# Per-head RMS norm in the attention fronts: epsilon added by VectorE, rotation and learned factors on raw rows, the rms factor last, D's five heads rotated together

## The chip, the cores and the metric

One core of one Trainium2 chip. The metric is device time in microseconds (us) for one execution, median of three runs; times inside an execution come from one profiled execution of the hardware profiler. Engines: TensorE (PE, its weight loads PEld), VectorE (DVE), ScalarE (ACT), GpSimd (POOL), and the DMA queue that SyncE (SP) issues.

## The reference

Two layers of a hybrid encoder, sequence 512, width 1024, all float32. Each layer's mixer has four attention branches, each on its own projection of the normed input. All of them norm queries and keys per head before the scores:

```python
def rms(x, g):
    y = x * lax.rsqrt(jnp.mean(x * x, axis=-1, keepdims=True) + EPS)
    return y * g

# A, differential: 4 heads x 2 maps x 64     C, windowed, 8 query / 2 key heads of 64
q = rms(q, g_qk[0]); k = rms(k, g_qk[1])
# B, latent: rotated part of 32, plain part of 64, 8 heads
q_nope = rms(q[..., :64], g_qk[0, :64]); q_rope = rope(rms(q[..., 64:], g_qk[0, 64:]), pos)
k_nope = rms(kv[..., :64], g_qk[1, :64])
# D, two-axis rotation, 8 query / 2 key heads of 64
q = axial_rope(rms(q, g_qk[0]), row, col); k = axial_rope(rms(k, g_qk[1]), row, col)

def rope(x, pos):           # x1, x2: halves of the head
    return x * cos + concatenate([-x2, x1]) * sin
...
o = stack([o_a, o_b, o_c, o_d]); br = einsum('bsmc,mcd->bsmd', o, w_branch)
x = x + (sigmoid(gate) * br).sum(2) @ w_out
x = x + memory_xattn(...)                   # 4 heads, 256 memory tokens
x = x + square(relu(rms(x, g_mlp) @ w_up)) @ w_down
```

The factor 1/rms is one number per token and head. The rotation is linear within one head of one token, and the learned factors go by channel.

## The kernel before

Every large product is made of three matmuls (L177, L178, L179) on a rounded part and a rest of each operand. So each weight tile `wst` that arrives by DMA is split: ScalarE casts it to `whi` (L299), GpSimd subtracts to get `wlo` (L167, four instructions a tile). Activations are split the same way into `spl` tiles: a copy on ScalarE, a subtraction on VectorE (L167 too).

The mixer of a layer runs through twelve units in the order B 0 to 3, A 0 to 3, C 0 and 1, D 0 and 1. Each unit has a front and an attention; the front of the next unit is emitted behind the attention of the one before, with pieces of other work (gates and branch projections, tile `df`) between them as a string in the file deals them out. A front projects four blocks of 128 tokens (tile `dn`, 24 matmuls of 384 columns a block in A, C and D; 9 of 192 and 256 in B). ScalarE copies the block to a raw tile `tok` and squares it, VectorE sums the squares per head into `sf` (L415). Then come two halves of two blocks each: add epsilon (L311, in B L716 and L717) and raise to the power -0.5 (L312, in B L718) on GpSimd; on VectorE multiply by that factor (A L452, C and D L552, B L722 and L723), by the learned factors (A L454 with `ga`, D L557 with `gd`, B L725 and L727), rotate in B and D (the function `rope`: four products into tile `zr` at L584 or two in B, then L586 and L587); split into `spl` (copies on ScalarE, subtractions L167); TensorE transposes (L403, into `dn`), and the result is copied to `T` tiles (L172 on ScalarE, L174 on VectorE) as the scores need it. D rotates its four query heads and its key head in two calls.

The order of instructions on each engine is not that of the file: the framework's scheduler sets it when the program is built, from a simulated timeline, so that a shorter path at one place moves the rows of all engines around it. Each engine then runs its own rows in order and waits where an operand is missing.

## Time and profile before

| | before |
|---|---|
| runs, us | 2363.37, 2363.65, 2367.36; median 2363.65 |
| profiled execution, us | 2361.96 (span 2360.0 of it) |
| mean granted TensorE clock | 0.992 |
| TensorE busy | 2281.5 us, 97% |
| VectorE, ScalarE, GpSimd busy | 59%, 49%, 55% |
| data moved | 258.25 MB, mean 109 GB/s |

The span runs from the first to the last instruction of the profiled execution; 2 us lie outside it. Busy time counts an engine's instructions alone. A wait is given with what released it, as the semaphores show.

### The profile page before, as it was taken

The page shows a single profiled execution, that of the slowest core. Times are in us where ns is not written, and L with a number is a line of the kernel's source. Part 1 is how long each engine was busy: PE and PEld are TensorE (multiplying, and loading weights), DVE is VectorE, ACT ScalarE, POOL GpSimd, SP SyncE. Part 2 cuts the span into 40 slices and gives each one's busy share as a digit, 9 for nine tenths or more (in the row PEclk, how much of TensorE's full clock was granted, in tenths as well). Part 3 has the DMA queues.
Part 4 walks back from the last instruction along what each step waited for, and adds up shares of the span by engine and source line. Part 5 has one row for each costly group of instructions (what it writes and reads, how often), then busy time and mean ns, then how long its engine had stood idle before and what let it go on. Part 6 is the DMA issues. An engine that isn't in the chain of part 4 may idle for free.

```text
span 2360.0 us, 33643 instructions
## 1 busy us (share of the span) xinstructions
PE 2281.5 (97%) x12032; PEld 1966.0 (83%) x12032; DVE 1384.1 (59%) x2980; ACT 1151.8 (49%) x2253; POOL 1299.0 (55%) x1657
## 2 busy tenths in 40 slices
PE   8999999998999899999999998999989999999999
PEld 7888889887888888888888887898878878888887
DVE  7778666888975642222457786568879648222222
ACT  4556556655653543223345565566556546322321
POOL 7553544625465376666665435355353754766663
PEclk9999999999999999999999999999999999999999
DMA  5321342442454133333343214324425531323332
GB/s 185 108 94 57 102 138 66 127 154 84 147 179 155 54 99 98 98 92 96 111 134 101 83 46 127 113 79 134 136 92 168 171 131 56 106 91 97 98 93 77
DMA packets 88775, 258.25 MB, mean 109 GB/s; under 512 B 9704, under 2 KB 12392, under 8 KB 88608
## 3 DMA queue, kind: packets, MB, share of 16 engines
q1 hardware_dynamic: 88608, 256.10, 34.4%
q8 instruction: 95, 1.56, 0.3%
q14 instruction: 72, 0.59, 0.1%
HBM read 222.46 MB, written 33.60 MB: 109 GB/s over the span
## 4 chain that ended last, share of the span: by engine, by line
PE 83%; DVE 11%; POOL 2%; issue 1%; ACT 1%; DMA 1%; SPq 0%; POOLq 0%; ACTq 0%; DVEq 0%
PE dn L177 13%; PE dn L178 13%; PE dn L179 13%; PE df L177 10%; PE df L179 9%; PE df L178 9%; PE tr L476 3%; PE sc L177 1%; PE sc L179 1%; PE sc L178 1%; PE dn L403 1%; POOL wlo L167 1%; DVE pt L480 1%; DVE zr L584 1%; PE sc L624 1%
## 5 line engine op out<-in xcount | busy, mean ns | idle before, releaser
L167 POOL TENSOR_TENSOR wlo<-wst,whi 128x256 fp32r<-128x256 f32 (+3 forms) x1400 | 1071.0, 797 | 745.4 <-ACT whi L299 671.3
L299 ACT CAST whi<-wst 128x1024 fp32r<-128x1024 f32 (+3 forms) x350 | 348.8, 1003 | 640.8 <-PE dn L178 293.7
L177 PE MATMUL df<-s,whi 128*128 128x512 f32 (+1 forms) x967 | 381.0, 394 | 8.1 <-DVE zg L785 3.2
L179 PE MATMUL df<-s,wlo 128*128 128x512 f32 (+1 forms) x967 | 376.1, 389 | 1.3 <-POOL wlo L167 1.3
L178 PE MATMUL df<-s,whi 128*128 128x512 f32 (+1 forms) x967 | 374.3, 387 | 1.6 <-DVE s L167 1.6
L177 PE MATMUL dn<-whi,s 128*128 128x384 f32 (+4 forms) x768 | 264.8, 348 | 13.6 <-ACT s L348 7.7
L179 PE MATMUL dn<-whi,s 128*128 128x384 f32 (+4 forms) x768 | 263.3, 343 | 0.0
L178 PE MATMUL dn<-wlo,s 128*128 128x384 f32 (+4 forms) x768 | 263.1, 344 | 0.0
L177 PEld LDWEIGHTS df<-s,whi 128*128 128x128 f32 x967 | 181.7, 188 | 46.6 <-DVE yl L808 6.1
L179 PEld LDWEIGHTS df<-s,wlo 128*128 128x128 f32 x967 | 181.8, 188 | 38.4 <-POOL wlo L167 2.9
L178 PEld LDWEIGHTS df<-s,whi 128*128 128x128 f32 x967 | 181.9, 188 | 34.3 <-DVE s L167 2.2
L178 PE MATMUL dn<-s,whi 128*128 128x512 f32 (+1 forms) x529 | 197.1, 373 | 0.0
L179 PE MATMUL dn<-s,wlo 128*128 128x512 f32 (+1 forms) x529 | 196.9, 373 | 0.0
L177 PE MATMUL dn<-s,whi 128*128 128x512 f32 (+1 forms) x529 | 196.5, 374 | 0.0
L177 PEld LDWEIGHTS dn<-whi,s 128*128 128x128 f32 x768 | 146.8, 192 | 24.5 <-ACT s L348 7.7
L480 DVE TENSOR_TENSOR pt<-tr,pt 128x512 fp32r<-128x512 f32 (+1 forms) x224 | 142.7, 644 | 26.0 <-ACT pt L479 17.3
L178 PEld LDWEIGHTS dn<-wlo,s 128*128 128x128 f32 x768 | 147.2, 192 | 8.9 <-POOL wlo L167 0.2
L179 PEld LDWEIGHTS dn<-whi,s 128*128 128x128 f32 x768 | 146.8, 191 | 6.9
L479 ACT CAST pt<-tr 128x512 fp32r<-128x512 f32 (+1 forms) x224 | 121.8, 556 | 55.9 <-PE tr L476 54.3
L311 POOL TENSOR_SCALAR sf<-sf 128x8 f32<-128x8 f32 (+2 forms) x44 | 13.9, 316 | 241.3 <-DVE sf L415 239.5
L179 PEld LDWEIGHTS dn<-s,wlo 128*128 128x128 f32 x529 | 99.6, 188 | 17.9 <-POOL wlo L167 0.2
L178 PEld LDWEIGHTS dn<-s,whi 128*128 128x128 f32 x529 | 99.6, 188 | 17.8
(376 smaller groups left out, 4827.3 us busy)
## 6 DMA issues: line engine op xcount, KB each, us to landing
wst<-in_wts_dram SPq DMA_DIRECT2D x272, 512.0 KB, 3.5
wst<-in_wts_dram SPq DMA_DIRECT2D x64, 384.0 KB, 3.1
yl<-yz SPq DMA_DIRECT2D x48, 512.0 KB, 4.0
yz<-zg SPq DMA_DIRECT2D x64, 256.0 KB, 2.2
yz<-yl SPq DMA_DIRECT2D x48, 256.0 KB, 3.0
bias<-tscr SPq DMA_DIRECT2D x16, 320.0 KB, 3.3
yl<-yz SPq DMA_DIRECT2D x16, 256.0 KB, 3.1
bias<-tscr SPq DMA_DIRECT2D x8, 448.0 KB, 3.5
```

Source lines behind the costliest of these rows:

```text
L167: (eng or V).tensor_tensor(out=dst, in0=src, in1=f(hi), op=ALU.subtract)
L177: a = T.matmul(ps, lhsT=lh, rhs=rh, start=first, stop=False)
L178: T.matmul(ps, lhsT=lh, rhs=rl, start=False, stop=False)
L179: b = T.matmul(ps, lhsT=ll, rhs=rh, start=False, stop=last)
L299: chain("wh", A.copy(hi[:, :n], st[:, :n]))
L311: G.tensor_scalar(dst, src, add, None, op0=ALU.add)
L403: T.transpose(ps[:rows_, i * P:(i + 1) * P], s, idn)
L476: T.transpose(ps[:, kb * P:(kb + 1) * P], src[:, kb * P:(kb + 1) * P], idn)
L479: A.copy(hi, pv)
L480: V.tensor_tensor(out=lo, in0=pv, in1=f(hi), op=ALU.subtract)
L584: V.tensor_tensor(out=tmp[:, :, :, o:o + 16], in0=x[:, :, :, oo:oo + 16], in1=bc(tab[:, 1, b2, o:o + 16], 2, nh), op=ALU.mult)
L624: T.matmul(ps[:, :nk], lhsT=q, rhs=Tk[:, 0, kb0 * P:kb0 * P + nk], start=True, stop=False)
```

## The change

The epsilon adds of all fronts move from GpSimd to VectorE, and the power on GpSimd is emitted with a higher priority for the scheduler. In A, B and D the learned factors, and in B and D the rotation too, work on the raw rows; the multiplication by the per-head factor comes last, in C after the key's factor. D's five heads (four of queries, one of keys) are rotated in one call, for which tile `zr` grows from 512 to 640 columns.

```diff
     def rpow(dst, src, add, n):
-        G.tensor_scalar(dst, src, add, None, op0=ALU.add)
-        G.tensor_tensor(out=dst, in0=dst, in1=mhalf[:, :n], op=ALU.pow)
+        V.tensor_scalar(dst, src, add, None, op0=ALU.add)
+        with tc.high_priority():
+            G.tensor_tensor(out=dst, in0=dst, in1=mhalf[:, :n], op=ALU.pow)
...
     # front_A, half
-            V.tensor_tensor(out=qk, in0=qk, in1=bc(s.rearrange("p (t h) -> p t h", t=2), 3, 64), op=ALU.mult)
             for m in range(2):
                 V.tensor_tensor(out=kk[:, :, m], in0=kk[:, :, m], in1=bc(ga, 1, 2), op=ALU.mult)
+            V.tensor_tensor(out=qk, in0=qk, in1=bc(s.rearrange("p (t h) -> p t h", t=2), 3, 64), op=ALU.mult)
...
     # front_G (C and D), half
-            rpow(s, s, 64 * EPS, 10)
             qk = tk[:, :, :320].rearrange("p t (h d) -> p t h d", h=5)
-            V.tensor_tensor(out=qk, in0=qk, in1=bc(s.rearrange("p (t h) -> p t h", t=2), 3, 64), op=ALU.mult)
...
                 V.tensor_tensor(out=qk, in0=qk, in1=bc(gd, 1, 2), op=ALU.mult)
-                rope(qk[:, :, 0:4], dt_, j, 4, 2)
-                rope(qk[:, :, 4:5], dt_, j, 1, 2)
+                rope(qk, dt_, j, 5, 2)
+            rpow(s, s, 64 * EPS, 10)
+            V.tensor_tensor(out=qk, in0=qk, in1=bc(s.rearrange("p (t h) -> p t h", t=2), 3, 64), op=ALU.mult)
...
     # front_B
-            G.tensor_scalar(s3[:, :, 0:4], s3[:, :, 0:4], 64 * EPS, None, op0=ALU.add)
-            G.tensor_scalar(s3[:, :, 4:6], s3[:, :, 4:6], 32 * EPS, None, op0=ALU.add)
-            G.tensor_tensor(out=s, in0=s, in1=mhalf[:, :12], op=ALU.pow)
+            V.tensor_scalar(s3[:, :, 0:4], s3[:, :, 0:4], 64 * EPS, None, op0=ALU.add)
+            V.tensor_scalar(s3[:, :, 4:6], s3[:, :, 4:6], 32 * EPS, None, op0=ALU.add)
+            with tc.high_priority():
+                G.tensor_tensor(out=s, in0=s, in1=mhalf[:, :12], op=ALU.pow)
...
-            V.tensor_tensor(out=qk, in0=qk, in1=bc(s3[:, :, 0:4], 3, 64), op=ALU.mult)
-            V.tensor_tensor(out=qr, in0=qr, in1=bc(s3[:, :, 4:6], 3, 32), op=ALU.mult)
...
             rope(qr, bt_, j, 2, 1)
+            V.tensor_tensor(out=qk, in0=qk, in1=bc(s3[:, :, 0:4], 3, 64), op=ALU.mult)
+            V.tensor_tensor(out=qr, in0=qr, in1=bc(s3[:, :, 4:6], 3, 32), op=ALU.mult)
...
     # rope
-        tmp = tl("zr", [P, S])[:, :2 * nh * w].rearrange("p (t h d) -> p t h d", t=2, h=nh)
+        tmp = tl("zr", [P, 640])[:, :2 * nh * w].rearrange("p (t h d) -> p t h d", t=2, h=nh)
```

GpSimd's order in layer 0, front A, unit 1, second half, before: `sf580` is the half's sums, `wlo645` to `wlo654` are weight rests of the next unit.

```order
L167 TENSOR_TENSOR wlo645_3567<-wst643_3564,whi644_3566 128x192 x4
L167 TENSOR_TENSOR wlo648_3576<-wst646_3573,whi647_3575 128x192 x4
L311 TENSOR_SCALAR sf580_3256<-sf580_3256 128x8
L167 TENSOR_TENSOR wlo651_3585<-wst649_3582,whi650_3584 128x192 x4
L312 TENSOR_TENSOR sf580_3256<-sf580_3256,mhalf_72 128x8
L167 TENSOR_TENSOR wlo654_3594<-wst652_3591,whi653_3593 128x192 x4
```

And now, at the same place:

```order
L167 TENSOR_TENSOR wlo645_3567<-wst643_3564,whi644_3566 128x192 x4
L167 TENSOR_TENSOR wlo648_3576<-wst646_3573,whi647_3575 128x192 x4
L313 TENSOR_TENSOR sf580_3256<-sf580_3256,mhalf_72 128x8
L167 TENSOR_TENSOR wlo651_3585<-wst649_3582,whi650_3584 128x192 x4
L167 TENSOR_TENSOR wlo654_3594<-wst652_3591,whi653_3593 128x192 x4
```

The add is gone from here, and the power has moved ahead of the four subtractions of `wlo651`.

VectorE's order in layer 0, front D, unit 0, second half, before: `sf1153` are its sums, `tok1152` its raw rows; `pt`, `zg`, `T1145` and `spl1158` belong to other stages and to the first half.

```order
L415 TENSOR_REDUCE sf1153_6116<-dn1154_6122 128x5
L480 TENSOR_TENSOR pt1110_5903<-tr1118_5930,pt1109_5902 128x3x128
L167 TENSOR_TENSOR spl1158_6171<-tok1148_6053,spl1158_6171 128x2x128
L785 TENSOR_TENSOR zg1173_6270<-df1172_6245,Rrow_95 128x512
L480 TENSOR_TENSOR pt1120_5943<-tr1124_5954,pt1119_5942 128x3x128
L174 COPY T1145_6026<-dn1160_6182 128x2x256
L480 TENSOR_TENSOR pt1120_5943<-tr1128_5970,pt1119_5942 128x3x128
L552 TENSOR_TENSOR tok1152_6115<-tok1152_6115,sf1153_6116 128x640
L557 TENSOR_TENSOR tok1152_6115<-tok1152_6115,gd_85 128x640
L584 TENSOR_TENSOR zr1162_6198<-tok1152_6115,ropd_t_87 128x8x16 x4
L586 TENSOR_TENSOR tok1152_6115<-tok1152_6115,ropd_t_87 128x2x256
L587 TENSOR_TENSOR tok1152_6115<-tok1152_6115,zr1162_6198 128x2x256
```

And now, from the rotation's first products to the split (the reduction and the multiply by `gd` stand ahead of these rows):

```order
L584 TENSOR_TENSOR zr1161_6188<-tok1152_6115,ropd_t_87 128x10x16 x3
L481 TENSOR_TENSOR pt1110_5903<-tr1118_5930,pt1109_5902 128x3x128
L584 TENSOR_TENSOR zr1161_6188<-tok1152_6115,ropd_t_87 128x10x16
L311 TENSOR_SCALAR sf1153_6116<-sf1153_6116 128x10
L586 TENSOR_TENSOR tok1152_6115<-tok1152_6115,ropd_t_87 128x640
L786 TENSOR_TENSOR zg1171_6256<-df1170_6231,Rrow_95 128x512
L174 COPY T1145_6026<-dn1159_6175 128x2x256
L587 TENSOR_TENSOR tok1152_6115<-tok1152_6115,zr1161_6188 128x640
L481 TENSOR_TENSOR pt1120_5943<-tr1124_5954,pt1119_5942 128x3x128
L481 TENSOR_TENSOR pt1120_5943<-tr1128_5970,pt1119_5942 128x3x128
L559 TENSOR_TENSOR tok1152_6115<-tok1152_6115,sf1153_6116 128x640
L167 TENSOR_TENSOR spl1162_6198<-tok1152_6115,spl1162_6198 128x8x64
```

The factor (L559) has gone behind the rotation and is the last step ahead of the split. On GpSimd the power of this half stands behind the same four weight subtractions before and now.

TensorE's order in layer 0, front D, unit 1, second half, around its first transposes (L403, now L404), before:

```order
L476 MATMUL tr1236_6521<-idr_68,p1234_6515 128x128 x4
L624 MATMUL sc1255_6600<-T1146_6027,T1145_6026 128x512
L625 MATMUL sc1255_6600<-T1146_6027,T1145_6026 128x512
L403 MATMUL dn1306_6902<-idr_68,spl1304_6896 128x128 x4
L403 MATMUL dn1307_6908<-idr_68,spl1304_6896 128x128 x4
L624 MATMUL sc1261_6626<-T1146_6027,T1145_6026 128x512
```

And now:

```order
L648 MATMUL pv1200_6387<-pt1212_6431,v1143_6024 128x256
L404 MATMUL dn1302_6874<-idr_68,spl1300_6868 128x128 x4
L404 MATMUL dn1303_6880<-idr_68,spl1300_6868 128x128 x4
L624 MATMUL sc1253_6586<-T1146_6027,T1145_6026 128x512
L625 MATMUL sc1253_6586<-T1146_6027,T1145_6026 128x512
L477 MATMUL tr1234_6507<-idr_68,p1232_6501 128x128 x4
L177 MATMUL df1318_6966<-s17_149,whi1316_6959 128x512
```

The transposes now come earlier. Between the last projection matmul and them stood 60 matmuls of fill (`df`), 16 of scores, 24 of values and 24 of transposes of `p`, and 12 of other blocks of the front; now there are 36, 12, 24, 20 and 12. In layer 0, front B, unit 1, the same count for the first half falls too: its transposes come ahead of work that was in front of them.

## Rows read from the trace of the kernel before

**Rows 1.** The page: the line of the span, and from part 1 the line of all engines, each with busy us, share of the span, and instructions (PE is TensorE, PEld its weight loads, DVE VectorE, ACT ScalarE, POOL GpSimd).

```profile
span 2360.0 us, 33643 instructions
...
PE 2281.5 (97%) x12032; PEld 1966.0 (83%) x12032; DVE 1384.1 (59%) x2980; ACT 1151.8 (49%) x2253; POOL 1299.0 (55%) x1657
```

**Rows 2.** TensorE's waits over the whole span, by its tile and line and by what it waited for: total us, times, longest us.

```profile
PE dn L403 <- DVE spl L167: 18.9, 7, 5.4
...
PE dn L403 <- ACT spl L732: 2.8, 3, 1.1
...
PE dn L403 <- ACT T L172: 2.1, 2, 1.8
PE dn L403 <- DVE T L174: 2.1, 5, 0.5
```

**Rows 3.** The timeline of TensorE at four places of the two layers. The columns are the start in us, the duration in us, engine, line, operation, output<-inputs with their shapes, the count of instructions that the row joins, and in brackets the engine's idle time before it with what ended it.

```profile
298.20 0.72 PE L403 MATMUL dn<-jr,spl 128*128 128x128 f32 x4 [3.83 <-DVE spl L167]
...
551.65 1.23 PE L403 MATMUL dn<-idr,spl 128*128 128x128 f32 x8 [5.42 <-DVE spl L167]
...
1471.15 0.72 PE L403 MATMUL dn<-jr,spl 128*128 128x128 f32 x4 [3.81 <-DVE spl L167]
...
1724.02 1.23 PE L403 MATMUL dn<-idr,spl 128*128 128x128 f32 x8 [3.88 <-DVE spl L167]
```

**Rows 4.** Busy time by stretch: the stretch in us, its length, busy us of TensorE, its weight loads, VectorE, ScalarE and GpSimd (instructions), then the granted clock of TensorE as a share of full speed, the DMA engines' busy share, and GB/s.

```profile
298.20:303.30 5.10, 4.73 (x21) 4.38 (x22) 3.56 (x10) 1.40 (x3) 1.06 (x1) 0.51 0.52 162
551.60:559.30 7.70, 7.14 (x29) 6.92 (x30) 2.63 (x6) 0.90 (x2) 0.00 (x0) 0.50 0.23 67
1471.10:1477.50 6.40, 5.98 (x25) 5.66 (x26) 3.62 (x10) 1.41 (x4) 1.06 (x1) 0.51 0.40 130
1713.30:1720.10 6.80, 6.75 (x34) 5.55 (x34) 4.75 (x8) 2.08 (x4) 5.29 (x5) 1.00 0.45 120
1724.00:1730.10 6.10, 5.58 (x24) 5.34 (x25) 2.59 (x6) 0.90 (x2) 0.00 (x0) 0.51 0.26 86
```

**Rows 5.** The timeline of GpSimd, of ScalarE and of VectorE in layer 0, front A, unit 1, second half.

```profile
290.64 0.25 POOL L311 TENSOR_SCALAR sf<-sf 128x8 f32<-128x8 f32 x1
290.97 2.28 POOL L167 TENSOR_TENSOR wlo<-wst,whi 128x192 fp32r<-128x192 f32 x4
293.20 1.67 POOL L312 TENSOR_TENSOR sf<-sf,mhalf 128x8 f32<-128x8 f32 x1
...
293.36 0.84 ACT L299 CAST whi<-wst 128x768 fp32r<-128x768 f32 x1 [2.48 <-POOL wlo L167]
...
295.07 0.90 DVE L452 TENSOR_TENSOR tok<-tok,sf 128x512 f32<-128x512 f32 x1
...
296.50 1.22 DVE L454 TENSOR_TENSOR tok<-tok,ga 128x128 f32<-128x128 f32 x2
```

**Rows 6.** The timeline of GpSimd and of VectorE in layer 0, front D, unit 0, second half.

```profile
538.46 2.28 POOL L167 TENSOR_TENSOR wlo<-wst,whi 128x192 fp32r<-128x192 f32 x4
540.71 1.98 POOL L312 TENSOR_TENSOR sf<-sf,mhalf 128x10 f32<-128x10 f32 x1
...
537.29 0.47 DVE L415 TENSOR_REDUCE sf<-dn 128x5 f32<-128x320 f32 x1
...
542.72 1.22 DVE L552 TENSOR_TENSOR tok<-tok,sf 128x640 f32<-128x640 f32 x1 [1.81 <-POOL sf L312]
...
545.11 1.59 DVE L584 TENSOR_TENSOR zr<-tok,ropd_t 128x128 f32<-128x128 f32 x4
...
547.73 0.96 DVE L587 TENSOR_TENSOR tok<-tok,zr 128x512 f32<-128x512 f32 x1
...
550.81 0.69 DVE L167 TENSOR_TENSOR spl<-tok,spl 128x512 fp32r<-128x512 f32 x1
```

**Rows 7.** The timeline of TensorE and of VectorE in layer 0, front D, unit 1, second half.

```profile
578.54 0.33 PE L179 MATMUL dn<-whi,s 128*128 128x384 f32 x1
...
579.64 0.40 PE L179 MATMUL df<-s,wlo 128*128 128x512 f32 x1
579.88 0.40 PE L177 MATMUL df<-s,whi 128*128 128x512 f32 x1
...
605.17 0.79 PE L403 MATMUL dn<-idr,spl 128*128 128x128 f32 x8
...
604.26 0.68 DVE L167 TENSOR_TENSOR spl<-tok,spl 128x512 fp32r<-128x512 f32 x1
```

**Rows 8.** The timeline of TensorE and of VectorE in layer 0, front B, unit 1, first half.

```profile
103.47 0.28 PE L179 MATMUL dn<-whi,s 128*128 128x256 f32 x1
...
122.89 0.78 PE L403 MATMUL dn<-idr,spl 128*96 128x128 f32 x8
...
109.81 0.68 DVE L722 TENSOR_TENSOR tok<-tok,sf 128x512 f32<-128x512 f32 x1
...
118.99 0.53 DVE L167 TENSOR_TENSOR spl<-tok,spl 128x128 fp32r<-128x128 f32 x1
```

**Rows 9.** Groups of VectorE's instructions by line and shape: count, busy us, mean ns of one, idle time before them.

```profile
L671 DVE TENSOR_SCALAR sf<-sf 128x1 f32<-128x1 f32 x8 | 1.2, 145 | 0.0
```

**Rows 10.** The timeline of GpSimd and of VectorE in layer 0, front D, unit 0, first half.

```profile
521.25 1.99 POOL L312 TENSOR_TENSOR sf<-sf,mhalf 128x10 f32<-128x10 f32 x1
...
521.40 0.67 DVE L167 TENSOR_TENSOR s<-of,s 128x512 fp32r<-128x512 f32 x1
```

More of the change, by code (lines that the diff above doesn't have):

```diff
@@ L836, in mem_prep @@
                 else:
-                    q = tl("zr", [P, S])[:, :NM]
+                    q = tl("zr", [P, 640])[:, :NM]
                     A.activation(q, st[:, k, :], AF.Square)
```

## The prediction, made before the changed kernel was timed

> **What bounds the kernel.** The page comes first: TensorE is busy for 97% of the span [rows 1], so only what it loses can be won. Its waits show where that is. The first transposes of a front's half (L403, the step that needs the split tile) wait for VectorE's split (18.9 us in 7 waits), for ScalarE's copy (2.8), and for an earlier transpose's result (2.1 and 2.1) [rows 2]: 25.9 us together. The timeline puts most of it at four places [rows 3]: the second half of front A's unit 1 and of front D's unit 0, in each layer. There it waits 3.8 to 5.4 us and then does something more: in the stretch behind each of the four the granted clock is 0.50 to 0.51, the lower level of 1.2 GHz, where the other 1.8 us wait (1713.3) is followed by 1.00 [rows 4]. The engine had been idle before each of the four. With a granted clock of 0.5, half of the stretch is lost: 5.10 x 0.49 = 2.5, 7.70 x 0.50 = 3.85, 6.40 x 0.49 = 3.1 and 6.10 x 0.49 = 3.0, in all 12.4 us. So all that the fronts cost TensorE is 25.9 + 12.4 = 38.3 us, and no rewriting of their normalisation can win more. The rest of its time is matmuls that the change doesn't touch.
>
> Next, why these four are late. Front A, unit 1: the eps add waits at 290.64 on GpSimd for its place between two weight splits, then four weight subtractions of 2.28 us stand between it and the power, which runs 293.20 to 294.87; only then VectorE's rms multiply (295.07, 0.90), the two multiplies by the learned factor (296.50, 1.22) and the split [rows 5]. TensorE ran out of other work at 298.20 - 3.83 = 294.37 [rows 3]. Front D, unit 0: the power ends at 542.69 and everything is behind it on VectorE: the multiply (1.22), from 543.94 the learned factors, the rotations and others, until the split at 550.81 [rows 6]. Fill work ended at 551.65 - 5.42 = 546.23 [rows 3].
>
> **The change part by part.**
>
> *Factors and rotation ahead of the power.* This takes VectorE's work off the path from the power to the split. In A's unit 1 the multiplies of 1.22 us go; in D's unit 0 the 6.87 us from 543.94 to 550.81 become a queue that starts at 537.76, when the reduction of the squares is done [rows 6].
>
> *The power with priority.* In A's unit 1 the order now has it behind the second weight's subtractions and ahead of the third's, about where the add stood: 290.6 + 1.67 = 292.3 instead of 294.87 [rows 5]. The multiply then ends at 293.2. But ScalarE's order has a weight cast (293.36, 0.84) in front of the copy [rows 5], so the copy (about 0.4) begins at 294.2 and the split is there near 295.0. Rest of the stall: some 0.8 of 3.8. In layer 1 the changed order of TensorE has one microsecond less of other work there (four to five 512-column matmuls); I take 2.0. Gain: 3.83 - 0.8 + 2.5 = 5.5 and 3.81 - 2.0 + 3.1 = 4.9. The half-clock stretch goes because a wait of 1.8 us left the clock at 1.00 [rows 4].
>
> *D's unit 0.* On GpSimd the power keeps its place behind the four subtractions [rows 6], and so ends near 542.7 as before. VectorE from 537.76 has, in the new order, six instructions for other stages (some 3.8 us of the 0.5 to 0.7 us kind), the eps add, and the merged rotation of 3.0 to 3.8 us (the rows' 1.59, about 1 and 0.96 for four heads, times 5/4 [rows 6]; up to a fifth less where no weight subtraction runs beside it). So the multiply starts near 545, not 542.72 + a queue behind it; it ends near 546.3, copy and split take 1.3 more: 547.6 to 548 against a slot of 546.23. Rest of the stall 1.8, no half clock. Gain: 5.42 - 1.8 + 3.85 = 7.5 in layer 0; 3.88 - 1.5 + 3.0 = 5.4 in layer 1, and 0.8 of the 1.82 us wait of its first half [rows 2].
>
> *The small waits.* What is left on the first two lines of [rows 2] (18.9 less the four is 2.0, in front A's unit 0 above all; 2.8 behind ScalarE's copy of the rotated part in front B) comes in waits of 1.1 us at most, shorter than the rotation or the factors that leave their paths: 3.5 of 4.8.
>
> *Eps add on VectorE, D's five heads at once.* An add on VectorE of such a size is near L671's 145 ns [rows 9]; 84 more come to 12 us over a VectorE that is busy for 59% [rows 1], and the merged rotation gives back 48 instructions. Nothing of this is on the path except 0.15 us a half, which the GpSimd add (0.25, and its place in the queue) [rows 5] outweighs. If the cover were gone: 24 halves a layer at 0.15, 3.6 us.
>
> *What the change takes away.* The order changes with it: the schedule puts the transposes of other halves earlier, so less of TensorE's work covers them. Front D's unit 1, second half: between the last projection matmul (578.54) and the first transposes (605.17) [rows 7] the order had 60 fill matmuls and now has 36, and 4 score matmuls and 4 transposes fewer. At 0.24 us from one 512-column matmul to the next (579.64, 579.88 [rows 7]) that is 28 x 0.24 + 0.4 = 7.1 us less of a cover of 26.3, while the split ended at 604.26 + 0.68, at the last moment. What leaves its path is the key head's rotation and what was queued behind the factors, some 4 to 5 us: a new stall of 2 in layer 0 and 1 in layer 1, where the front starts with more in hand. Front B, priced the same way from the order, loses cover in nearly every half: unit 1's first half from 19.1 us (103.75 to 122.89 [rows 8]) to 11.7, unit 2's second from 20.7 to 13.3, the others 0 to 6. Their path becomes shorter: in unit 1, from the multiply (109.81) to the last split's end (118.99 + 0.53) it was 9.7 us [rows 8], with rotation and factors among attention's instructions; the multiplies, copies and splits that stay need about 3.5. The split is then ready near 113, 9.3 us after the projection, inside 11.7. As VectorE's queue differs from half to half I take 3 us of new stalls in layer 0 and 2 in layer 1, not 0 (the bound if all are like unit 1) and not 42 (the sum of all cover lost in front B, if nothing became shorter).
>
> **Sum.** 5.5 + 4.9 + 7.5 + 5.4 + 0.8 + 3.5 = 27.6, less 2 + 1 + 3 + 2 = 8: about 20 us off the profiled 2361.96, so 2342; the median of the runs is 1.7 above the profiled one and I take 2342 as it stands, with some of the follow-on waits (0.5 and less) on the gain's side.
>
> **A rule against it.** The rotations and factors are TENSOR_TENSOR with both inputs in SBUF, and they now run beside the power on GpSimd. The trace has that pair once: the power at 521.25 for 1.99 us and VectorE's split beside it, at 521.40, for 0.67 [rows 10], the same as L167's 0.68 at 604.26 without it [rows 7]. So the power does not hold VectorE up. The Trainium skill, "SBUF — State Buffer", section "Who interferes with whom", says that a VectorE instruction with two SBUF inputs contends with a GpSimd one that reads SBUF, and that whoever is first fully blocks the other. By that page every raw multiply beside a power would wait up to its 2 us; the trace disagrees for the power. By that rule the raw work of the four halves would only move behind the power and their stalls stay: about 2362, for which I give 0.04, as part of the second rival below.
>
> **The rivals.** *Nearly all is won* (0.12): the covers that shrink still suffice, ScalarE's copy comes past the weight cast; then 32 to 38 of the 38.3 us go: about 2326. For it: unit 1 of front B has 2 us to spare. Against it: D's unit 0, where VectorE's queue ends after the slot whatever GpSimd does.
> *Little is won* (0.20): the split isn't ready much earlier, since in D's unit 0 the power keeps its place, or VectorE is held beside it (0.04 of the 0.20), and front B's shrunk covers take the rest: gain 0 to 12, about 2356.
> *Slower* (0.12): the new covers are shorter than the new paths, and each of the new waits brings its own half-clock stretch. D's unit 1 with 7.1 - 2.5 = 4.6 of stall and 3.0 of clock, twice, makes 15; front B's four halves with the largest loss (7.3, 6.1, 7.4, 4.9, less 2 each for the shorter path) make 17.7 and four times 2.5: 43 against 27.6, so some 15 us slower, 2377. It decides where the lost cover exceeds what leaves the path by over 3 us a half, for then the clock goes down too. Against it: the 9.7 us in front B that shrink to 3.5.
> *The forecast* (0.56): gain 12 to 32, 2330 to 2350.
>
> **Range and chances.** A measurement here can tell about 0.2%, 4.7 us. Faster by more: the forecast and the first rival, with half of the second: 0.56 + 0.12 + 0.09 = 0.77. Within: 0.11, from the second. Slower: 0.12. The range goes from the first rival's 2325 to no change, 2362: what is left out is the slower case and a little below.
>
> **What would show it.** In the changed profile: waits of the transposes on VectorE's split near 8 us instead of 18.9; no half-clock stretch behind A's unit 1 and D's unit 0; the power in A's unit 1 before the third weight's subtractions; VectorE's merged rotation before the multiply. Wrong, if TensorE waits at D's unit 1 or in front B for over 3 us and the granted clock is 0.5 behind it, or if the multiply in D's unit 0 still waits for the power at 542.7.

## The result, and the profile after

| | before | changed |
|---|---|---|
| median of 4 runs, us | 2365.51 (2363.37 to 2367.7) | 2343.98 (2338.22 to 2347.62) |
| profiled execution, us | 2361.96 | 2338.22 |
| mean granted TensorE clock, profiled | 0.992 | 0.997 |

The ratio of the runs is 0.9907, 95% interval 0.9883 to 0.993: 22 us faster, where 2342 us were forecast. The changed kernel's profiled execution is the fastest of its four; the others granted 0.992 to 0.994. The profiled execution of the kernel before is a good one too: in 50 later executions it granted 0.987 to 0.991, where the profile has 0.992.

The page of the changed kernel, the same two lines as [rows 1]:

```profile
span 2336.4 us, 33592 instructions
...
PE 2270.5 (97%) x12032; PEld 1957.0 (84%) x12032; DVE 1398.3 (60%) x3016; ACT 1145.9 (49%) x2253; POOL 1283.9 (55%) x1573
```

TensorE's idle time (span less busy) fell from 78.5 to 65.9 us, and its busy time by 11.0 at the same count of matmuls: that is the clock. Of the 23.7 us between the two profiled executions 12.6 are idle time and 11.0 are matmuls that ran faster.

TensorE's waits in the changed kernel (total us, times, longest us; L403 is now L404), to be read against [rows 2]:

```profile
PE df L177 <- DVE zg L786: 8.1, 12, 2.1
...
PE tr L477 <- DVE pt L481: 4.7, 6, 1.5
PE pv L648 <- DVE pt L481: 4.1, 5, 1.4
...
PE dn L404 <- ACT T L172: 3.2, 4, 1.1
PE dn L404 <- DVE T L174: 2.9, 5, 1.0
...
PE dn L404 <- DVE spl L167: 1.0, 1, 1.0
...
PE dn L404 <- ACT spl L734: 0.7, 1, 0.7
```

Three lines of the kernel before that [rows 2] doesn't have:

```profile
PE df L177 <- DVE zg L785: 3.2, 7, 1.2
...
PE tr L476 <- DVE pt L480: 2.0, 3, 1.0
...
PE pv L648 <- DVE pt L480: 0.5, 2, 0.2
```

The waits for the split are nearly gone (18.9 us in 7 waits before, 1.0 in one now; ScalarE's copy 2.8 before, 0.7 now). Part of it came back elsewhere: fill matmuls wait 8.1 us for VectorE's gate product `zg` (3.2 before), and transposes and value products wait 4.7 and 4.1 us for VectorE's copies of `p` (2.0 and 0.5 before). The transposes' waits for earlier results rose by 1.9 us. So 20.0 us went and 13.1 came back in these lines; the rest of the 12.6, 5.7 us, is small waits elsewhere that went.

Four stretches behind the former stalls, and one that is left (columns as in [rows 4]):

```profile
292.00:297.00 5.00, 4.28 (x28) 3.98 (x29) 4.19 (x9) 2.01 (x5) 3.02 (x5) 1.00 0.74 209
538.80:546.50 7.70, 6.75 (x44) 6.36 (x43) 4.76 (x8) 2.91 (x6) 2.40 (x5) 1.00 0.56 172
1448.30:1454.70 6.40, 5.14 (x32) 4.37 (x32) 5.64 (x11) 3.67 (x8) 5.15 (x7) 1.00 0.67 229
1692.80:1700.50 7.70, 7.11 (x38) 5.98 (x38) 5.55 (x9) 3.91 (x7) 7.16 (x9) 1.00 0.39 113
780.00:786.90 6.90, 6.25 (x33) 6.25 (x34) 4.00 (x8) 1.48 (x4) 0.00 (x0) 0.51 0.24 76
```

Where the granted clock was 0.50 to 0.51 [rows 4], it is 1.00 now; in a second profile of the same order of rows (x_noprio below) it is 1.00 at these four places too. The stretch at 780.0 lies in the cross-attention, which had one before too.

### The profile page after: what moved, and what is told of

The parts are those of the page before. It is cut to its first block, busy times and chain, and to the rows that moved or that the text cites. A ratio compares the mean times of both kernels' runs of the same rounds, so it can differ in the third digit from the quotient of the medians.

```text
span 2336.4 us, 33592 instructions
## 1 busy us (share of the span) xinstructions
PE 2270.5 (97%) x12032; PEld 1957.0 (84%) x12032; DVE 1398.3 (60%) x3016; ACT 1145.9 (49%) x2253; POOL 1283.9 (55%) x1573
## 4 chain that ended last, share of the span: by engine, by line
PE 81%; DVE 10%; issue 4%; POOL 3%; ACT 1%; DMA 1%; SPq 0%; POOLq 0%; ACTq 0%; DVEq 0%
PE dn L177 12%; PE dn L178 12%; PE dn L179 12%; PE df L177 10%; PE df L178 10%; PE df L179 10%; PE tr L477 3%; POOL wlo L167 2%; PE dn L404 1%; DVE pt L481 1%; PE sc L177 1%; PE sc L179 1%; PE sc L178 1%; DVE spl L167 1%; PE sc L624 1%
## 5 line engine op out<-in xcount | busy, mean ns | idle before, releaser
L167 POOL TENSOR_TENSOR wlo<-wst,whi 128x256 fp32r<-128x256 f32 (+3 forms) x1400 | 1083.2, 807 | 713.2 <-ACT whi L299 642.4
L177 PE MATMUL df<-s,whi 128*128 128x512 f32 (+1 forms) x967 | 381.0, 394 | 13.1 <-DVE zg L786 8.1
L313 POOL TENSOR_TENSOR sf<-sf,mhalf 128x8 f32<-128x8 f32 (+2 forms) x44 | 72.7, 1652 | 223.4 <-DVE sf L311 208.5
```

The lines of the kernel that those rows point to most:

```text
L167: (eng or V).tensor_tensor(out=dst, in0=src, in1=f(hi), op=ALU.subtract)
L177: a = T.matmul(ps, lhsT=lh, rhs=rh, start=first, stop=False)
L313: G.tensor_tensor(out=dst, in0=dst, in1=mhalf[:, :n], op=ALU.pow)
```

## The experiments

Each was timed beside the kernel before; the ratio is to those executions of the kernel before, and a median in the first column belongs to its own series. Idle is the page's span less TensorE's busy time; clock is what 1 - mean granted clock comes to over the span, both of the profiled execution; rest is the span less both. The last column is the clock figure as a mean over all executions that were timed (50 of the kernel before, 4 to 12 of the others), each of which records its span and granted clock.

| kernel | median us | ratio, 95% interval | span | idle us | clock us | rest us | clock us, all runs |
|---|---|---|---|---|---|---|---|
| before | 2365.51 | | 2360.0 | 78.5 | 18.9 | 2262.6 | 26.7 |
| changed | 2343.98 | 0.9907 (0.9883 to 0.993) | 2336.4 | 65.9 | 7.0 | 2263.5 | 14.1 |
| x_raw | 2348.51 | 0.9928 (0.9915 to 0.9941) | 2346.6 | 68.5 | 14.1 | 2264.0 | 14.6 |
| x_add | 2371.75 | 1.0027 (1.0014 to 1.004) | 2367.6 | 78.5 | 28.4 | 2260.7 | 31.2 |
| x_noprio | 2341.07 | 0.9897 (0.9883 to 0.9911) | 2337.2 | 64.3 | 11.7 | 2261.2 | 12.6 |
| x_rope41 | 2344.31 | 0.9912 (0.9898 to 0.9925) | 2342.5 | 68.1 | 11.7 | 2262.7 | 13.1 |
| x_onlyD | 2353.07 | 0.9943 (0.9928 to 0.9957) | 2350.4 | 69.6 | 21.2 | 2259.6 | 20.8 |
| x_onlyA | 2361.74 | 0.9975 (0.9966 to 0.9983) | 2359.1 | 73.2 | 28.3 | 2257.6 | 26.4 |
| x_onlyB | 2366.36 | 0.9997 (0.9988 to 1.0005) | 2366.5 | 82.7 | 23.7 | 2260.1 | 23.6 |
| x_AD | 2351.5 | 0.9929 (0.9915 to 0.9943) | 2350.5 | 69.9 | 21.2 | 2259.4 | 19.7 |
| x_ABD | 2344.7 | 0.9911 (0.9897 to 0.9924) | 2342.5 | 65.7 | 16.4 | 2260.4 | 17.6 |
| x_ACD | 2358.09 | 0.9967 (0.9955 to 0.9979) | 2354.1 | 68.5 | 25.9 | 2259.7 | 27.1 |

The rest is 2257.6 to 2264.0 us in all twelve. So two numbers of a page, TensorE's idle time and its granted clock, tell the time of every variant within some 3 us; a cost smaller than that could hide. The clock of one execution is a poor measure of a kernel, though: the profiled execution of the kernel before lost 18.9 us, its 50 others 26.7 in the mean. What a variant does to the clock is read from the last column: the whole change wins some 13 us there, D alone 6, A alone nothing, and the adds alone lose 4.5.

### x_raw: the order of factors alone

```diff
     def rpow(dst, src, add, n):
-        V.tensor_scalar(dst, src, add, None, op0=ALU.add)
+        G.tensor_scalar(dst, src, add, None, op0=ALU.add)
...
-            V.tensor_scalar(s3[:, :, 0:4], s3[:, :, 0:4], 64 * EPS, None, op0=ALU.add)
-            V.tensor_scalar(s3[:, :, 4:6], s3[:, :, 4:6], 32 * EPS, None, op0=ALU.add)
+            G.tensor_scalar(s3[:, :, 0:4], s3[:, :, 0:4], 64 * EPS, None, op0=ALU.add)
+            G.tensor_scalar(s3[:, :, 4:6], s3[:, :, 4:6], 32 * EPS, None, op0=ALU.add)
```

The diff is against the changed kernel; the power's priority is out too (an empty context stands in its place), which x_noprio shows to do nothing.

> Factors and rotation on raw rows and the merged rotation as in the changed kernel, but the epsilon adds back on GpSimd. On GpSimd the add and the power of front A unit 1 stand in the old places again (the power behind the third weight's subtractions). Theory (each of two parts wins one of the two stalls): front D unit 0 stays without a stall, because there the order of factors does it; front A unit 1 keeps its late power and only saves the 1.22 us of the learned factor, so it waits about 2.6 us in each layer, perhaps with a half-clock stretch behind it: 3 to 8 us slower than the changed kernel, about 2347 to 2352 us. Rival (the order of factors wins all, the add's engine does nothing): no slower than the changed kernel by over 2 us, 2346 us or less.

Measured 2348.51 us, inside the theory's 2347 to 2352. GpSimd and TensorE in layer 0, front A, unit 1, second half:

```profile
287.64 0.25 POOL L311 TENSOR_SCALAR sf<-sf 128x8 f32<-128x8 f32 x1
287.97 2.27 POOL L167 TENSOR_TENSOR wlo<-wst,whi 128x192 fp32r<-128x192 f32 x4
290.20 1.67 POOL L313 TENSOR_TENSOR sf<-sf,mhalf 128x8 f32<-128x8 f32 x1
...
294.40 0.52 PE L404 MATMUL dn<-jr,spl 128*128 128x128 f32 x4 [3.15 <-DVE spl L167]
```

The add stands in its old place, four subtractions of 2.27 us follow, and the power begins at 290.20, as far behind the add as in [rows 5]. TensorE waits 3.15 us there and 1.80 in layer 1, where the theory had 2.6 each, with half-clock stretches behind both; front D's unit 0 waits for its split no more. So the order of factors wins D's stall and most of the whole (17 us), and the add's move wins A's: x_noprio, timed in the same series, differs by the add's engine alone and is 7 us faster.

### x_add: the adds on VectorE alone

```diff
     def rpow(dst, src, add, n):
-        G.tensor_scalar(dst, src, add, None, op0=ALU.add)
+        V.tensor_scalar(dst, src, add, None, op0=ALU.add)
         G.tensor_tensor(out=dst, in0=dst, in1=mhalf[:, :n], op=ALU.pow)
...
-            G.tensor_scalar(s3[:, :, 0:4], s3[:, :, 0:4], 64 * EPS, None, op0=ALU.add)
-            G.tensor_scalar(s3[:, :, 4:6], s3[:, :, 4:6], 32 * EPS, None, op0=ALU.add)
+            V.tensor_scalar(s3[:, :, 0:4], s3[:, :, 0:4], 64 * EPS, None, op0=ALU.add)
+            V.tensor_scalar(s3[:, :, 4:6], s3[:, :, 4:6], 32 * EPS, None, op0=ALU.add)
```

This diff is against the kernel before.

> The epsilon adds on VectorE, but the rms factor first, then learned factors and rotation, D in two calls, as in the kernel before. Theory: the power of front A unit 1 comes some 2.5 us earlier, so its wait falls from 3.8 to 1 to 1.5 us with no half-clock stretch behind it; front D unit 0 still waits 4 to 5.4 us in layer 0 and 3.9 in layer 1 for VectorE's split, each with a granted clock near 0.5 behind it. So about 12 us (8 to 16) faster than the kernel before, about 2352 us. Rival (the add's engine wins all): 2344 us as the changed kernel. Second rival (it wins nothing): 2364 us.

Measured 1.0027: slower, by 5 us over the kernel before, and none of the three had that. The part on D held, its unit 0 still waits:

```profile
552.48 1.23 PE L404 MATMUL dn<-idr,spl 128*128 128x128 f32 x8 [4.39 <-DVE spl L167]
```

In layer 0 the wait of A's unit 1 fell to 1.53 us as the theory said, but in layer 1 it was 4.27, and A's unit 2 waits 1.48 and 1.51 us where it had not waited. GpSimd, VectorE and TensorE in layer 1, front A, unit 1:

```profile
1468.50 1.66 POOL L313 TENSOR_TENSOR sf<-sf,mhalf 128x8 f32<-128x8 f32 x1
1470.10 4.48 POOL L167 TENSOR_TENSOR wlo<-wst,whi 128x192 fp32r<-128x192 f32 x8
...
1470.20 4.93 DVE L453 TENSOR_TENSOR tok<-tok,sf 128x512 f32<-128x512 f32 x1 [0.84 <-POOL sf L313]
...
1476.62 0.72 PE L404 MATMUL dn<-jr,spl 128*128 128x128 f32 x4 [4.27 <-DVE spl L167]
```

The power ends at 1470.16. VectorE's multiply by the rms factor, which waited for it, begins at 1470.20, and GpSimd has begun its next eight subtractions at 1470.10, back to back for 4.48 us. The multiply, 0.90 us in [rows 5], takes 4.93 and ends 0.55 us behind that train. Three more rms multiplies in this trace, each begun beside such a train (front C's beside one of six), took 3.74, 3.52 and 3.48 us. So a power that comes earlier, with a long train of subtractions right behind it, can shut VectorE out until the train ends. It isn't certain to: in layer 0 the same multiply came as late (290.36, the train at 290.28) and took 1.07, and there the train took 5.58 us instead of 4.48. The changed kernel has trains of eight and twelve at such places too, and no multiply of front A takes over 1.17 us there; what decides between the two isn't settled. In the kernel before four subtractions at most followed a power at this place. Over the whole span the idle time is that of the kernel before (78.5 us): what some waits lost others won. The 5 us are in the clock, 31.2 us against 26.7 over all runs.

### x_noprio: without the priority

```diff
-        with tc.high_priority():
+        with ExitStack():
             G.tensor_tensor(out=dst, in0=dst, in1=mhalf[:, :n], op=ALU.pow)
```

The same edit was made in front B.

> The changed kernel without the priority of the power. The order of the rows on every engine is then the same, row for row, as that of the changed kernel, so theory: the same time, 2344 us within 3, and as a second profile of the same rows it shows how much of a run's difference (2338 to 2348 us) is half-clock stretches: mean granted clock and time go together, about 2 us for each 0.001. Rival (the priority does something that the order does not show): over 5 us slower, the powers later.

The order of all five engines is the same row for row, and so is the time: 2341.07 us. The priority does nothing in this program; that the power stands earlier is the work of the add's leaving GpSimd. The profiled execution waits where the changed kernel's does (the split 1.1 us, the gate product 8.3) but lost 11.7 us by the clock instead of 7.0: the same rows give different half-clock stretches from run to run, and the spread of the changed kernel's runs goes with it (0.997 at 2338 us, 0.992 at 2348).

### x_rope41: D's rotation in two calls

```diff
-                rope(qk, dt_, j, 5, 2)
+                rope(qk[:, :, 0:4], dt_, j, 4, 2)
+                rope(qk[:, :, 4:5], dt_, j, 1, 2)
```

> The changed kernel with D's rotation in two calls, four heads and one, as before. VectorE has 48 short instructions more, about 3.8 instead of 2.9 us a half, and TensorE's order has some 25 us instead of 17 us of other work in front of the second half's transposes in D unit 1. Theory: the 0.9 us a half matter little, front D unit 0 has about 1 us more of a stall in each layer, and VectorE's late copies in D unit 1 of layer 0 (1.49 and 1.37 us) go: within 4 us of the changed kernel. Rival (the merged rotation is what removes D's stalls): 5 to 12 us slower, with waits of over 3 us and a half-clock stretch in D unit 0.

Measured 2344.31 us, as the changed kernel within its interval; against x_noprio it is 3 us more. TensorE's idle time is 2 to 4 us more, among it a wait of 1.61 us at front D's unit 0, first half. That TensorE's late operands from VectorE in layer 0, D's unit 1, would go was wrong: it waits 1.60 us there for the attention's output (`of`) and 0.82 for a copy of `p`.

### x_onlyD, x_onlyA, x_onlyB: one front at a time

In front D alone, front A alone, front B alone, the adds, the order of factors and (in D) the rotation are those of the changed kernel; all else is the kernel before. `rpow` takes the add's engine as an argument, GpSimd if none is given. For front A, and then for D's branch of its function (C keeps the rows of the kernel before); in B the edit is that of the change shown above:

```diff
-            rpow(s, s, 64 * EPS, 8)
+            rpow(s, s, 64 * EPS, 8, V)
...
-            V.tensor_tensor(out=qk, in0=qk, in1=bc(s.rearrange("p (t h) -> p t h", t=2), 3, 64), op=ALU.mult)
             for m in range(2):
                 V.tensor_tensor(out=kk[:, :, m], in0=kk[:, :, m], in1=bc(ga, 1, 2), op=ALU.mult)
+            V.tensor_tensor(out=qk, in0=qk, in1=bc(s.rearrange("p (t h) -> p t h", t=2), 3, 64), op=ALU.mult)
...
-                rpow(s, s, 64 * EPS, 10)
-                V.tensor_tensor(out=qk, in0=qk, in1=sb, op=ALU.mult)
                 V.tensor_tensor(out=qk, in0=qk, in1=bc(gd, 1, 2), op=ALU.mult)
-                rope(qk[:, :, 0:4], dt_, j, 4, 2)
-                rope(qk[:, :, 4:5], dt_, j, 1, 2)
+                rope(qk, dt_, j, 5, 2)
+                rpow(s, s, 64 * EPS, 10, V)
+                V.tensor_tensor(out=qk, in0=qk, in1=sb, op=ALU.mult)
```

> The kernel before with the change in front D alone (add on VectorE, raw rows, one rotation of five heads); A, B and C as before. TensorE's order is that of the kernel before up to front D; unit 1's second half has 7 us less of other work in front of its transposes. Theory (the ledger by units adds up): the waits of D unit 0 (5.42 and 0.51 in layer 0; 1.82, 3.88 and 0.50 in layer 1) and the half-clock stretches behind them (3.85 and 3.0) go but for about 2, and unit 1 gets 2 to 3 us of new waits on VectorE: 12 to 15 us faster than the kernel before, A unit 1's waits of 3.8 us unchanged. Rival (the gain comes from elsewhere, a changed order of all engines): less than 5 us faster.

Measured 0.9943, 13.5 us (10 to 17 by the interval): the theory. D's share of the transposes' waits is gone, and over all runs the clock lost 20.8 us where the kernel before lost 26.7; what is left of the waits is A's:

```profile
PE dn L403 <- DVE spl L167: 9.8, 4, 4.2
```

> The kernel before with the change in front A alone. Theory: unit 1's second half waits about 1 us instead of 3.83 and 3.81 and has no half-clock stretch (2.5 and 3.1), unit 0's 0.9 goes: 10 to 13 us faster than the kernel before; D unit 0 waits 4 to 5.4 us as before, with a granted clock near 0.5 behind it. Rival (as with the adds alone: VectorE's multiply is shut out by a train of weight subtractions right behind the power and takes 3 to 5 us): 3 to 5 us of waits in A's units and 0 to 5 us of gain.

Measured 0.9975, 6 us, half of the theory. The wait itself came out as expected, 1.02 us in layer 0 and 1.06 in layer 1; the rival's shut-out did not occur. But a half-clock stretch came all the same. TensorE's timeline, and the stretches ahead of and in the drop:

```profile
295.38 0.51 PE L403 MATMUL dn<-jr,spl 128*128 128x128 f32 x4 [1.02 <-DVE spl L167]
```

```profile
295.30:297.50 2.20, 1.44 (x13) 1.23 (x13) 2.20 (x4) 1.14 (x3) 2.20 (x4) 1.00 0.85 233
297.60:301.10 3.50, 3.50 (x12) 3.30 (x11) 2.59 (x7) 0.84 (x3) 1.38 (x3) 0.51 0.84 261
```

Front D's unit 0 still waits, 3.46 and 3.43 us in its second halves, and 2.73 in layer 0's first half, which had not waited. Over the whole span the idle time fell by 5.3 us, and over all runs the clock lost as much as in the kernel before (26.4 and 26.7 us): the 6 us are idle time alone.

> The kernel before with the change in front B alone; the other work in front of B's transposes falls as in the changed kernel (unit 1's first half from 19.0 to 11.7 us, unit 2's second from 20.7 to 13.3). Theory by the profile of the changed kernel, where B's transposes wait for the split once, 0.7 us: the 1.1 us waits of unit 0 go and VectorE's gate product comes late by 1.4 us twice: within 3 us of the kernel before. Rival (the prediction's 5 us of new waits in B): 3 to 6 us slower; second rival (the shorter front pays): 4 us or more faster.

Measured 0.9997 (0.9988 to 1.0005): no difference, as the theory had it. So the cover that front B loses (up to 7.4 us a half) is not paid, and its shorter path is not paid out either.

### x_AD, x_ABD, x_ACD: the fronts together

The edits of the single fronts put together; in C the learned factor of the key comes first and the rms multiply last, with the add on VectorE:

```diff
-                rpow(s, s, 64 * EPS, 10)
-                V.tensor_tensor(out=qk, in0=qk, in1=sb, op=ALU.mult)
                 V.tensor_tensor(out=kk, in0=kk, in1=bc(gc, 1, 2), op=ALU.mult)
+                rpow(s, s, 64 * EPS, 10, V)
+                V.tensor_tensor(out=qk, in0=qk, in1=sb, op=ALU.mult)
```

> The kernel before with the change in fronts A and D, B and C as before. Theory: the gains of the two add up, 22 to 27 us faster than the kernel before, as fast as the changed kernel within 4 us. Rival (front B's part or C's is needed too): 6 us or more slower than the changed kernel.

Measured 0.9929, 17 us (13 to 20): A and D alone make 5.9 + 13.5 = 19.4, inside the interval, and the whole change 22 to 24. So their gains add up as far as can be told, but the theory fell: some 5 us are missing to the changed kernel and 7 to x_noprio, whose interval lies clear of this one. A wait that the changed kernel doesn't have, layer 0, in the second half of front A's unit 0, just ahead of unit 1 (VectorE, TensorE):

```profile
251.94 0.69 DVE L454 TENSOR_TENSOR tok<-tok,sf 128x512 f32<-128x512 f32 x1
252.66 0.69 DVE L787 TENSOR_TENSOR zg<-df,Rrow 128x512 f32<-128x512 f32 x1
...
253.41 0.50 PE L177 MATMUL df<-s,whi 128*128 128x512 f32 x1 [2.03 <-DVE zg L787]
```

The gate product `zg` stands in VectorE's order behind that half's rms multiply (251.94), and fill matmuls of TensorE wait 2.03 us for it.

> The kernel before with the change in fronts A, B and D, C as before. Fronts A and D together were 17 us faster than the kernel before, the whole change 22 to 25, front B alone 1. Theory (what is missing comes with front B: its earlier transposes move the start of front A, and with it VectorE's gate products that TensorE waits for by 2.0 us twice in the kernel with A and D): within 2 us of the changed kernel, some 2342 to 2346 us, and the 2.0 us waits at the start of front A's unit 1 go. Rival (it comes with front C): about 2351 us, as with A and D.

Measured 0.9911, 21 us, 2344.7 us: as the changed kernel. The two waits of 2.03 us are gone, the idle time is 4.2 us less than with A and D, the clock's loss 2.1 over all runs.

> The kernel before with the change in fronts A, C and D, B as before. Theory (what is missing comes with front B): about 2351 us, as with A and D alone, with the waits of 2.0 us for VectorE's gate product at the start of front A's unit 1. Rival (it comes with front C, whose learned factor now lies before the power): 2342 to 2346 us, and the waits of 1.7 and 2.9 us for VectorE's output sum in front of front D's unit 0 go.

Measured 0.9967: slower than A and D without C, by some 9 us, which neither theory had. Its idle time is 1.4 us less than with A and D; over all runs its clock lost 27.1 us against 19.7. The waits for the output sum stayed (2.08 and 2.45 us). So front B's part is needed where C's is there: without it the ratio is 0.9967, with it 0.9907 (x_noprio 0.9897), 14 to 17 us, and nearly all of that is clock, though B alone does nothing. With A and D and without C it is worth some 4 us (0.9929 to 0.9911), which the intervals don't set apart. Front C's part costs where B's is absent and nothing where it is there (changed kernel against x_ABD: within the intervals); C alone wasn't run. Why the clock falls more often in the one order than in the other isn't settled.

## Why the prediction was right, step by step

**The bound and the sum.** The bound held: all that the fronts cost was put at 38.3 us, waits and half clock about two to one. The gain of about 20 was 7 us of waits (15 won, 8 lost) and 12.4 of half clock. Measured were 12.6 and 11.0 in the two profiles. So both parts are there, and the four half-clock stretches went as forecast. That the sum came within 2 us is in part luck, as its terms by fronts did not come out so well: A's make 12 and A alone won 6, D's make 10.7 and D alone won 13.5, B's make a loss of some 3 and B alone lost nothing, front C had no term, and the fronts don't add (17 us for A and D, 8 for A, C and D, 22 for all).

**Front A, unit 1.** Layer 0 came out to two tenths of a microsecond. GpSimd, VectorE, ScalarE and TensorE in the changed kernel:

```profile
287.30 1.64 POOL L313 TENSOR_TENSOR sf<-sf,mhalf 128x8 f32<-128x8 f32 x1
288.90 5.48 POOL L167 TENSOR_TENSOR wlo<-wst,whi 128x192 fp32r<-128x192 f32 x8
...
283.72 0.93 DVE L454 TENSOR_TENSOR tok<-tok,ga 128x128 f32<-128x128 f32 x2 [0.17 <-ACT tok L413]
...
288.98 1.07 DVE L455 TENSOR_TENSOR tok<-tok,sf 128x512 f32<-128x512 f32 x1 [1.12 <-POOL sf L313]
...
290.02 0.83 ACT L299 CAST whi<-wst 128x768 fp32r<-128x768 f32 x1 [2.30 <-PE df L178]
290.76 0.40 ACT L458 CAST spl<-tok 128x256 fp32r<-128x256 f32 x1
...
292.04 0.51 PE L404 MATMUL dn<-jr,spl 128*128 128x128 f32 x4 [1.02 <-DVE spl L167]
```

The factor (283.72) is done before the power. TensorE's slot is 292.04 - 1.02 = 291.02. Against it, the power ends 2.1 us ahead (forecast 294.37 - 292.3 = 2.1), the multiply 1.0 ahead (forecast 1.2), ScalarE's weight cast stands in front of its copy, which begins 0.3 ahead (forecast 0.2), and the stall is 1.02 (forecast 0.8). In layer 1 no wait for the split is left, where 2.0 were forecast; transposes of this unit wait 1.07 and 0.95 us there for copies of earlier transposes' results. What was put down to the priority is the add's doing (x_noprio).

**Front D, unit 0** was sized too small. Forecast were stalls of 1.8 and 1.5 us; the split's transposes don't wait at all:

```profile
533.14 2.54 POOL L313 TENSOR_TENSOR sf<-sf,mhalf 128x10 f32<-128x10 f32 x1
...
526.70 0.47 DVE L416 TENSOR_REDUCE sf<-dn 128x5 f32<-128x320 f32 x1
...
535.72 1.21 DVE L559 TENSOR_TENSOR tok<-tok,sf 128x640 f32<-128x640 f32 x1 [0.92 <-POOL sf L313]
537.67 1.57 DVE L167 TENSOR_TENSOR spl<-tok,spl 128x512 fp32r<-128x512 f32 x2 [0.74 <-ACT spl L562]
...
522.33 0.62 ACT L562 CAST spl<-tok 128x512 fp32r<-128x512 f32 x1
...
523.17 0.52 ACT L413 ACTIVATE tok<-dn,r_mix 128x320 f32<-128x320 f32 x1
...
538.84 0.80 PE L404 MATMUL dn<-idr,spl 128*128 128x128 f32 x8
```

The power ends at 535.68 and multiply and split follow in 3 us, half a microsecond more than worked out. The forecast had VectorE's queue as the last to be done, after the power. It took what it was given: VectorE was through with it at 535.72 - 0.92 = 534.80, 7.6 us after the reduction's end, where some 7.2 were forecast. (The rotation alone was mis-sized: its rows make 4.4 us, or 3.5 less a fifth, not 3.0 to 3.8, and it measured 4.25 here; the eps add took 0.56 us and not 0.15.) But the power was the last, and the multiply waits 0.92 us for it. The prediction's own list has such a wait as a sign of being wrong; nothing is lost by it here, as the transposes at 538.84 wait for nothing. What was missed lies ahead of the queue. The projection's last matmul ended some 5.3 us before the reduction at 526.70, against 8.2 us in the kernel before, because ScalarE's copy of the last block stood behind the first half's split copy in both orders, and that copy was late before. ScalarE there, before:

```profile
532.45 0.62 ACT L562 CAST spl<-tok 128x512 fp32r<-128x512 f32 x1 [2.52 <-DVE tok L587]
...
533.70 0.53 ACT L412 ACTIVATE tok<-dn,r_mix 128x320 f32<-128x320 f32 x1
```

The first half's split copy waited 2.5 us for the last rotation (532.45), and the copy of the last block's raw rows came 4.6 us after its matmuls had ended at 529.09; in the changed kernel these are 522.33 and 523.17, 1.8 us after 521.40. A shorter path in one half brought the statistics of the next half forward through ScalarE's queue, by 2.9 us against the projection, which is more than the 1.8 of stall that was forecast. D alone won 13.5 us, against the 10.7 that the sum's terms for D make (7.5 + 5.4 + 0.8 - 3); the interval (10 to 17) holds both.

**Front D, unit 1.** The forecast of new waits, 2 and 1 us, had the place but not the object. The transposes there don't wait for the split; attention does, for VectorE's copies of `p`, which now stand behind rotation and factors:

```profile
574.93 0.66 PE L477 MATMUL tr<-idr,p 128*128 128x128 f32 x4 [1.49 <-DVE pt L481]
...
577.45 0.39 PE L648 MATMUL pv<-pt,v 128*128 128x256 f32 x1 [1.37 <-DVE pt L481]
```

In layer 1 it is 0.64 and 1.20 us, so 2.9 and 1.8 in all. Raw work that moves ahead on its own path moves ahead of other work on the same engine. The largest of the gate product's waits is the same thing in D's unit 0, layer 1 (VectorE, then TensorE):

```profile
1687.23 1.28 DVE L584 TENSOR_TENSOR zr<-tok,ropd_t 128x160 f32<-128x160 f32 x2
...
1690.26 0.81 DVE L586 TENSOR_TENSOR tok<-tok,ropd_t 128x640 f32<-128x640 f32 x1
1691.10 1.10 DVE L587 TENSOR_TENSOR tok<-tok,zr 128x640 f32<-128x640 f32 x1
1692.12 0.68 DVE L786 TENSOR_TENSOR zg<-df,Rrow 128x512 f32<-128x512 f32 x1
...
1692.85 0.50 PE L177 MATMUL df<-s,whi 128*128 128x512 f32 x1 [2.08 <-DVE zg L786]
```

Four products of the rotation and L586 and L587 stand in front of `zg`, and TensorE waits 2.08 us for it. The rise of `zg` and `p` waits over the span (4.9, 2.7 and 3.6 us) stands where the sum had 8 us of new stalls in D's unit 1 and in B: 11 against 8, and the waiting instructions were others. The 5.7 us of small waits that went elsewhere, for which the sum had no term, made up for it.

**Front B**, taken at 5 us of loss beside some 2 us won in its small waits, cost nothing alone, and with A, C and D it wins 14 us or more (x_ACD), which the sum had nothing for. The two bounds (0 and 42) were far apart, and the row taken, unit 1's first half, spoke for the lower one. Of the small waits of A and B together (4.8 us, 3.5 forecast as won) 4.1 went.

**The clock.** That no half-clock stretch follows a stall of 1.8 us or less was drawn from one row (the wait at 1713.3 [rows 4]). It held in the changed kernel's profile, where even the 2.08 us at 1692.85 are followed by 1.00, and fell in x_onlyA, where a wait of 1.02 us is followed by 3.5 us at 0.51. So the outcome held at the four places, in two profiles; the rule that it was drawn from did not, and that the sum came out is luck here. A alone won 6 us and not the 12 that its terms make (5.5, 4.9 and some 1.5 of the small waits): its idle time fell by 5.3 us where these have some 6, and its clock terms (2.5 and 3.1) did not come, as over all runs its clock lost what that of the kernel before lost.

**The rivals.** Slower did not come, but x_add shows that it lay near: the same power, moved forward without the order of factors, made the kernel 5 us slower. The rule of the Trainium skill, "SBUF — State Buffer", section "Who interferes with whom", was set aside with one pair of rows. The prediction calls it the only such pair in that trace, and it isn't: in layer 1 the same power (1694.94, 1.99 us) and split (1695.10, 0.67) stand beside each other, with the same result. For the power the changed kernel's trace says so too (GpSimd's powers and VectorE's rotations beside them, two places in layer 0, front D, unit 1):

```profile
556.61 1.95 POOL L313 TENSOR_TENSOR sf<-sf,mhalf 128x10 f32<-128x10 f32 x1 [15.21 <-DVE sf L311]
...
557.30 0.81 DVE L586 TENSOR_TENSOR tok<-tok,ropd_t 128x640 f32<-128x640 f32 x1
...
574.83 3.18 POOL L313 TENSOR_TENSOR sf<-sf,mhalf 128x10 f32<-128x10 f32 x1
...
575.40 0.80 DVE L586 TENSOR_TENSOR tok<-tok,ropd_t 128x640 f32<-128x640 f32 x1
```

L586 begins 0.69 us into the first power and takes 0.81 us, 0.80 beside the second; the first power takes 1.95 us. For a power, then, the trace still disagrees with the rule, as VectorE isn't blocked; the second power takes 3.18 us, and what lengthened it no row shows. Beside GpSimd's subtractions it is another matter. Where the rule speaks of the one that comes first and fully blocks the other, the trace agrees in x_add, where the multiply beside a train of them took 4.93 us; in the changed kernel (288.98, begun 0.08 us behind such a train) it took 1.07. So the price, where it came, lay with the subtractions behind the power and not with the power, and the prediction had weighed the rule at the power alone.

## What to carry to other kernels

Work that doesn't need a late factor goes ahead of it where the engine is idle anyway; but on an engine with one queue look at what is queued behind the moved work, for that is who waits next. A step that is taken off a shared queue moves all the queue's other rows: count what follows right behind the step that remains, not only what stood ahead of it (x_add). Compare the granted clock over many executions and not in one profile of each kernel. Where a scheduler sets the order, change one front at a time as well as all, since the gains don't add.

## What the runs showed of the hardware

- A VectorE multiply of two SBUF operands that took 0.90 us in the kernel before took 4.93 in x_add beside a train of eight GpSimd subtractions (4.48 us) that had begun 0.1 us before it; in layer 0 of the same trace it took 1.07 and the train 5.58.
- The granted clock can fall to 0.51 behind a wait of 1.02 us (x_onlyA) and stay at 1.00 behind one of 1.02 or 2.08 (changed kernel) and of 1.82 (before). What decides it isn't settled here. Two profiles of the same order of rows lost 7.0 and 11.7 us by it, and twelve profiles of the same count of matmuls 7.0 to 28.4.
